# Expert selection: all queries first, the choices cut into pieces between the turned blocks, more low parts on GpSimd

## The chip, the cores and the metric

One Trainium2 chip, one of its cores, one launch. The time is the device time of one execution in microseconds (us). The engines have short names in the profile: PE is TensorE's matmul, PEld its weight load, DVE VectorE, ACT ScalarE, POOL GpSimd, SP SyncE, which issues most transfers.

## What is computed

A stack of blocks on one sequence of 256 tokens of width 1024: a gated delta rule, a gated MLP, a sliding-window attention, a second MLP, a block with a convolution and an attention, and at the end a layer of 16,384 experts. The change touches only that last layer:

```
q = (hc @ w_query).reshape(TOKEN_CHUNK, PEER_HEADS, 2, PEER_HALF)
sc = jnp.einsum('thpd,pnd->thpn', q, sub_keys)
vals, idx = lax.top_k(sc, PEER_TOPK)
cand = vals[:, :, 0, :, None] + vals[:, :, 1, None, :]
...
top_s, pos = lax.top_k(cand, PEER_TOPK)
gate = jax.nn.softmax(top_s, axis=-1)
u = expert_u[expert_idx]
act = jax.nn.gelu(jnp.einsum('thkd,td->thk', u, hc))
vv = expert_v[expert_idx]
return jnp.einsum('thk,thkd->td', gate * act, vv)
```

There are 8 heads, 128 keys in each half and 16 experts chosen for each head and token. The kernel gathers nothing: it computes the activation of all 16,384 experts for all tokens, as 128 blocks of 128 experts, and multiplies it with gates that are zero where an expert was not chosen.

## The kernel before

Every large product is made of three matmuls (`mm3`): each operand is split into a rounded high part and a low part, the rest. For weights ScalarE rounds the high part (`wh`) and VectorE or GpSimd subtracts to get the low part (`wl`). `low` deals the low parts out by a string for each stage, `LOW`: in the stage "top" it was "PPPD", three on GpSimd and one on VectorE, in turn.

The experts' layer, `peer`, has four stretches. In the first, "top", the queries are projected and scored (`peer_scores`, one call for each head), each head's best 16 of each half and of the pairs are found (`peer_topk`), the choices are turned into tables of keys and gates (`peer_tables`), and the first 64 blocks of `expert_u` are read, turned and multiplied (`u_pair`, two blocks at a time). In the second, "up", `u_pair` does the other 64 blocks while the gates of the first are made (`gates`, `gated`). The last two run over `expert_v`.

`u_pair` takes a pair of blocks. `u_turned` loads a block with four transfers into `raw` (three buffers), VectorE turns it with one stream transpose into `rt` (three buffers), and ScalarE casts the high part `wh` (three buffers). Then one of the two low parts goes to VectorE and one to GpSimd (`wl`, three buffers). A copy of one element for each partition ("the small copy" below) writes into GpSimd's `wl` first, so that GpSimd can't start ahead of that place in VectorE's order. 48 matmuls follow, and ScalarE takes the GELU of the pair.

The Tile framework orders each engine's instructions at build time by a planner with a timeline of its own, and prefers what stands earlier in the program. `InOrder` wraps an engine so that its instructions keep the program's order. Before, it was used from the stretch "up" on; in "top" the planner mixed VectorE's choices, tables, turns and low parts freely. The order in the program was `PEER`: the query and the choice of each head in turn, then the eight steps of the tables, then the 32 pairs of blocks.

Of the kernel before, what the change touches and what calls it, by code (L numbers as in the profile page):

```python
# [21 lines left out]
P = 128  # L22
T = 256
# [53 lines left out]
PEER = " ".join([f"q{i} k{i}" for i in range(8)] + [f"T{i}" for i in range(8)] + [f"u{i}" for i in range(32)])  # L77
# [7 lines left out]
LOW = dict(gdn="PPD", ffn="PD", swa="PPD", mix="P", tail="PPD", top="PPPD", up="PD", down="D", last="D")  # L85


class InOrder:

    def __init__(self, tc, eng):  # L90
        self.tc, self.eng = tc, eng

    def __getattr__(self, name):
        f = getattr(self.eng, name)
        return lambda *a, **kw: self.tc.keep_in_program_order(f(*a, **kw))


class Net:
# [746 lines left out]
    def peer_scores(self, us, kp, st, h):  # L845
# [22 lines left out]
        st[h] = sc = t(kp, [P, 2, 2, P], "sc", bufs=2)  # L868
# [4 lines left out]
    def peer_topk(self, kp, st, h):  # L873
        nc, t = self.nc, self.t

        def top16(v, i, src):
            nc.vector.max(v[:, 0:8], src)
            nc.vector.max_index(i[:, 0:8], v[:, 0:8], src)
            nc.vector.match_replace(src, v[:, 0:8], src, -3e38)
            nc.vector.max(v[:, 8:16], src)  # L880
            nc.vector.max_index(i[:, 8:16], v[:, 8:16], src)

        vals, idx, tops, pos = st["top"]
        sc = st.pop(h)
# [12 lines left out]

    def peer_tables(self, kp, st, i):

        nc, t = self.nc, self.t  # L900
        _, idx, tops, pos = st["top"]
        io = st["io"]
        b, step = i // 4, i % 4
        if step == 0:
            e = t(kp, [P, 8, 16], "e")
            tb = tops[:, b]
            nc.vector.tensor_tensor(e, tb, tb[:, :, 0:1].to_broadcast([P, 8, 16]), op=ALU.subtract)
            nc.scalar.activation(e, e, AF.Exp)
            z = t(kp, [P, 8], "z")
            nc.vector.tensor_reduce(z, e, axis=AX.X, op=ALU.add)  # L910
            nc.vector.reciprocal(z, z)
            nc.vector.tensor_tensor(e, e, z.unsqueeze(2).to_broadcast([P, 8, 16]), op=ALU.mult)
            st["sel"] = sel = t(kp, [P, 3, P], "sel")
            nc.vector.tensor_copy(sel[:, 2, :], e.rearrange("t h k -> t (h k)"))

            pb = pos[:, b].rearrange("t h k -> t (h k)")
            st["at"] = t(kp, [P, P], "row", BF16), t(kp, [P, P], "low", BF16)
            for o, arg, op in zip(st["at"], (3, 7), (ALU.logical_shift_right, ALU.bitwise_and)):
                ab = t(kp, [P, P], "ab", U32)
                nc.vector.tensor_scalar(ab, pb, arg, None, op0=op)  # L920
                nc.vector.tensor_copy(o, ab)
        elif step < 3:
            p, (row, low) = step - 1, st["at"]
            abf = t(kp, [P, P], "abf", BF16)
            if p == 0:
                nc.vector.tensor_scalar(abf, row, -1.0, 0.0, op0=ALU.add, op1=ALU.max)
            else:
                nc.vector.tensor_scalar(abf, row, 1.0, 8.0, op0=ALU.is_equal, op1=ALU.mult)
                nc.vector.tensor_add(abf, abf, low)
            ixf = t(kp, [P, 8, 16], "ixf", BF16)  # L930
            nc.vector.tensor_copy(ixf, idx[:, b, :, p, :])
            n = P // 4
            for i in range(4):
                c, h = slice(i * n, (i + 1) * n), slice(2 * i, 2 * i + 2)
                eq = t(kp, [P, n, 16], "eq16", BF16)
                nc.vector.tensor_tensor(eq, abf[:, c].unsqueeze(2).to_broadcast([P, n, 16]),
                                        io.unsqueeze(1).to_broadcast([P, n, 16]), op=ALU.is_equal)
                eh = eq.rearrange("t (h k) a -> t h k a", h=2)
                nc.vector.tensor_tensor(eh, eh, ixf[:, h].unsqueeze(2).to_broadcast([P, 2, 16, 16]), op=ALU.mult)
                nc.vector.tensor_reduce(st["sel"][:, p, c], eq, axis=AX.X, op=ALU.add)  # L940
        else:
            ps = self.ps()
            for p in range(3):
                nc.tensor.transpose(ps[:, p * P : (p + 1) * P], st["sel"][:, p, :], self.ident)
            tk = slice(b * P, (b + 1) * P)

            ku = t(kp, [P, 2, P], "ku", U32, bufs=1)
            nc.vector.tensor_copy(ku, ps[:, 0:256].rearrange("k (p t) -> k p t", p=2))
            for i, (arg, op) in enumerate(((4, ALU.logical_shift_right), (15, ALU.bitwise_and))):
                kk = t(kp, [P, 2, P], "kk", U32, bufs=1)  # L950
                nc.vector.tensor_scalar(kk, ku, arg, None, op0=op)
                nc.vector.tensor_copy(st["part"][:, i, :, tk], kk)
            gf = t(kp, [P, P], "gf")
            nc.vector.tensor_copy(gf, ps[:, 256:384])

            ex = t(kp, [P, P], "ex", U32)
            nc.vector.tensor_scalar(ex, gf.bitcast(U32), 0x7F800000, None, op0=ALU.bitwise_and)
            ef = ex.bitcast(F32)
            nc.vector.tensor_scalar(ef, ef, 2.0 ** -116, None, op0=ALU.max)
            nc.vector.tensor_scalar(st["two"][:, tk], ef, 2.0 ** -10, None, op0=ALU.mult)  # L960
            nc.vector.tensor_scalar(ex, ex, 0x7F800000, None, op0=ALU.bitwise_xor)
            nc.vector.scalar_tensor_tensor(gf, gf, 512.0, ef, op0=ALU.mult, op1=ALU.mult)
            nc.vector.tensor_copy(st["gate"][:, 0, tk], gf)
            nc.vector.tensor_sub(st["gate"][:, 1, tk], gf, st["gate"][:, 0, tk])

    def peer(self):
# [6 lines left out]
        with tc.tile_pool(name="ba", bufs=1, **tile_) as ba, tc.tile_pool(name="us", bufs=3, **tile_) as us, \  # L973
# [9 lines left out]
            ve = [nc.vector]  # L983

            def u_turned(j):
# [5 lines left out]
                ve[0].transpose(rt, raw)  # L991
# [5 lines left out]
            def u_pair(j, buf, between=None):  # L997
# [6 lines left out]
                if between:  # L1004
                    between()
# [526 lines left out]
```

## Time and profile before

| | |
|---|---|
| time, median of 3 runs | 1987.35 us (1985.11 to 1990.6) |
| the profiled execution: its time | 1986.34 us |
| its span | 1984.6 us |
| PE busy | 1848.3 us, 93% |
| DVE busy | 1438.0 us, 72% |
| ACT busy | 956.5 us, 48% |
| POOL busy | 671.8 us, 34% |
| mean granted TensorE clock | 0.973 |

The busy shares are means over the whole span. The stretch that the change touches lies between 1072 and 1376 us; what stands in its rows counts, not the mean.

### The profile page before, as it was taken

How to read it: one execution, taken by the hardware profiler on the slowest of the kernel's cores; microseconds unless marked ns; L12 is line 12 of the kernel's file. 1: busy time of each engine (PE TensorE's matmuls, PEld its weight loads, DVE VectorE, ACT ScalarE, POOL GpSimd, SP SyncE). 2: the span in 40 equal slices, each digit the busy share in tenths (PEclk: the TensorE clock that was granted, in tenths of full speed). 3: DMA queues.
4: the chain of work that ended last, by engine and by line, in shares of the span. 5: the costliest groups of instructions: out<-in, count | busy, mean ns of one | idle time of the engine just before them, and what ended most of it. 6: DMA issues, size and time to landing. Idle time of an engine off the chain costs nothing. (4 is left out here: it accounts for less than half of the span.)

```text
span 1984.6 us, 36930 instructions
## 1 busy us (share of the span) xinstructions
PE 1848.3 (93%) x14537; PEld 1747.2 (88%) x14537; DVE 1438.0 (72%) x2765; ACT 956.5 (48%) x1419; POOL 671.8 (34%) x309
## 2 busy tenths in 40 slices
PE   7979999999899999999968978889999999999998
PEld 7879999999889999989968968779999988887886
DVE  6786656666546666588864799999888878875555
ACT  5744435555656555456444533433333443444443
POOL 4444333444323444655634423334333300000000
PEclk9989999999899999999979999999999999999999
DMA  6454236666424666443524555555555555555665
GB/s 198 118 160 139 86 107 201 191 192 193 134 86 128 212 192 185 135 139 108 170 86 139 161 128 149 140 137 160 155 161 154 149 170 160 163 159 169 195 195 171
DMA packets 243435, 306.29 MB, mean 154 GB/s; under 512 B 26076, under 2 KB 213821, under 8 KB 243133
## 3 DMA queue, kind: packets, MB, share of 16 engines
q1 hardware_dynamic: 240864, 302.84, 50.6%
q8 instruction: 114, 1.87, 0.4%
q10 hardware_dynamic: 2237, 1.07, 0.2%
q14 instruction: 60, 0.49, 0.1%
q0 software_dynamic: 160, 0.02, 0.0%
HBM read 298.60 MB, written 4.74 MB: 153 GB/s over the span
## 5 line engine op out<-in xcount | busy, mean ns | idle before, releaser
L233 POOL TENSOR_TENSOR wl<-raw,wh 128x1024 fp32r<-128x1024 f32 (+1 forms) x196 | 470.5, 2404 | 558.5 <-ACT wh L242 499.8
L242 ACT CAST wh<-raw 128x1024 fp32r<-128x1024 f32 (+1 forms) x285 | 297.8, 1047 | 319.2 <-issue 111.9
L233 DVE TENSOR_TENSOR wl<-raw,wh 128x1024 fp32r<-128x1024 f32 x233 | 294.4, 1264 | 162.2 <-ACT wh L1103 103.4
L251 PE MATMUL pp<-xh,wl 128*128 128x256 f32 x1392 | 394.5, 284 | 16.4 <-DVE wl L1009 16.3
L249 PE MATMUL pp<-xh,wh 128*128 128x256 f32 x1392 | 394.9, 284 | 15.1 <-DVE kq L491 10.3
L251 PE MATMUL pa<-xh,wl 128*128 128x256 f32 (+1 forms) x1336 | 382.0, 286 | 19.7 <-DVE wl L1009 19.6
L249 PE MATMUL pa<-xh,wh 128*128 128x256 f32 (+1 forms) x1336 | 382.9, 287 | 14.4 <-ACT hT L304 6.2
L250 PE MATMUL pp<-xl,wh 128*128 128x256 f32 x1392 | 393.1, 282 | 2.1 <-DVE xl L374 2.1
L250 PE MATMUL pa<-xl,wh 128*128 128x256 f32 (+1 forms) x1336 | 381.1, 285 | 2.0 <-DVE xl L374 1.9
L251 PEld LDWEIGHTS pp<-xh,wl 128*128 128x128 f32 x1392 | 267.0, 192 | 18.8 <-DVE wl L1009 18.3
L249 PEld LDWEIGHTS pp<-xh,wh 128*128 128x128 f32 x1392 | 267.1, 192 | 16.9 <-issue 10.7
L251 PEld LDWEIGHTS pa<-xh,wl 128*128 128x128 f32 (+1 forms) x1336 | 257.3, 193 | 22.4 <-DVE wl L1009 22.4
L249 PEld LDWEIGHTS pa<-xh,wh 128*128 128x128 f32 (+1 forms) x1336 | 257.3, 193 | 16.5 <-ACT hT L304 6.6
L250 PEld LDWEIGHTS pp<-xl,wh 128*128 128x128 f32 x1392 | 266.8, 192 | 2.5 <-DVE xl L374 2.3
L1009 POOL TENSOR_TENSOR wl<-rt,wh 128x1024 fp32r<-128x1024 f32 x64 | 166.0, 2594 | 291.1 <-ACT wh L994 209.2
L250 PEld LDWEIGHTS pa<-xl,wh 128*128 128x128 f32 (+1 forms) x1336 | 257.3, 193 | 3.2 <-DVE xl L374 2.4
L994 ACT CAST wh<-rt 128x1024 fp32r<-128x1024 f32 x128 | 134.3, 1049 | 240.6 <-PE pa L250 104.2
L1103 ACT CAST wh<-raw 128x1024 fp32r<-128x1024 f32 x128 | 135.0, 1055 | 216.4 <-PE pa L1113 210.1
L1112 PE MATMUL pa<-wl,rt 128*128 128x512 f32 x512 | 201.7, 394 | 0.0
L1113 PE MATMUL pa<-wh,rt 128*128 128x512 f32 x512 | 199.5, 391 | 0.0
L1111 PE MATMUL pa<-wh,rt 128*128 128x512 f32 x512 | 164.6, 394 | 1.4 <-ACT rt L1097 1.4
L1154 POOL TENSOR_TENSOR fsb<-fsb,mhalf 128x1 f32<-128x1 f32 x2 | 1.1, 550 | 393.8 <-DVE fsb L1153 393.8
(433 smaller groups left out, 3575.4 us busy)
## 6 DMA issues: line engine op xcount, KB each, us to landing
raw<-in_peer_u_dram SPq DMA_DIRECT2D x512, 128.0 KB
raw<-in_peer_v_dram SPq DMA_DIRECT2D x128, 512.0 KB
raw<-in_ffn_w_up_dram SPq DMA_DIRECT2D x88, 512.0 KB
raw<-in_a_w_in_dram SPq DMA_DIRECT2D x48, 512.0 KB
raw<-in_ffn_w_down_dram SPq DMA_DIRECT2D x44, 512.0 KB
raw<-in_w_in_dram SPq DMA_DIRECT2D x44, 512.0 KB
raw<-in_a_w_out_dram SPq DMA_DIRECT2D x16, 512.0 KB
raw<-in_peer_w_query_dram SPq DMA_DIRECT2D x16, 512.0 KB
```

The source lines that it names most:

```text
L233: (self.nc.vector if order[self.turn % len(order)] == "D" else self.nc.gpsimd).tensor_tensor(out, raw, high, op=ALU.subtract)
L242: nc.scalar.copy(wh, raw)
L249: mm(out, wh, xh, start=start, stop=False, skip_group_check=skip)
L250: mm(out, wh, xl, start=False, stop=False, skip_group_check=skip)
L251: mm(out, wl, xh, start=False, stop=stop, skip_group_check=skip)
L994: nc.scalar.copy(uh.rearrange("p f (b e) -> p f b e", b=4), rv)
L1009: eng.tensor_tensor(lo.rearrange("p f (b e) -> p f b e", b=4), rv, high.bitcast(F32).rearrange("p f (b e) -> p f b e", b=4), op=ALU.subtract)
L1103: nc.scalar.copy(vh, raw)
L1111: nc.tensor.matmul(o, w2[:, 0, i, s], vh[:, c], start=first, stop=False)
L1112: nc.tensor.matmul(o, w2[:, 0, i, s], vl[:, c], start=False, stop=False)
L1113: nc.tensor.matmul(o, w2[:, 1, i, s], vh[:, c], start=False, stop=last)
L1154: nc.gpsimd.tensor_tensor(o, o, self.mhalf(), op=ALU.pow)
```

## The change

- All eight calls of `peer_scores` stand first; `sc` gets eight buffers instead of two, so that no score waits for a choice.
- `peer_topk` and `peer_tables` become generators. Each `yield` ends a piece and names its cost in us. `spend` takes pieces until their costs reach a sum: 14.0 us (`HEAD`) ahead of the first pair; in the first 16 pairs (`BOTH`) 1.0 us after each of the two turns; in the other 16 pairs 2.6 us once, after both turns. What is left is done at the end.
- In those first 16 pairs both low parts go to GpSimd, with a small copy for each. In the other 16, one is VectorE's and one GpSimd's, as before.
- VectorE keeps the program's order through the whole stretch "top", not only from "up" on.
- The low parts of the queries all go to GpSimd (`top="P"`).
- The two halves' searches in `peer_topk` alternate. In `peer_tables` the cast of the indices and a copy out of PSUM move from VectorE to ScalarE, the comparisons are done on 64 columns at a time instead of 32, and one copy falls away.

```diff
-LOW = dict(gdn="PPD", ffn="PD", swa="PPD", mix="P", tail="PPD", top="PPPD", up="PD", down="D", last="D")
+BOTH, HEAD, PIECE = 16, 14.0, (1.0, 2.6)
+LOW = dict(gdn="PPD", ffn="PD", swa="PPD", mix="P", tail="PPD", top="P", up="PD", down="D", last="D")
...
-        st[h] = sc = t(kp, [P, 2, 2, P], "sc", bufs=2)
+        st[h] = sc = t(kp, [P, 2, 2, P], "sc", bufs=8)
...
+        def top16(*of):
+            for s in (slice(0, 8), slice(8, 16)):
+                for v, _, src in of:
+                    ve.max(v[:, s], src)
+                for v, i, src in of:
+                    ve.max_index(i[:, s], v[:, s], src)
+                if s.start == 0:
+                    for v, _, src in of:
+                        ve.match_replace(src, v[:, s], src, -3e38)
...
+            top16(*[(vals[:, b, h, p], idx[:, b, h, p], sc[:, b, p, :]) for p in range(2)])
+            yield 2.5
...
+            ve.tensor_tensor(cand[:, 0:2, :], va[:, 0:1].unsqueeze(2).to_broadcast([P, 2, 8]),
+                             vb.rearrange("t (a b) -> t a b", a=2), op=ALU.add)
+            ve.tensor_tensor(cand[:, 2:17, :], va[:, 1:16].unsqueeze(2).to_broadcast([P, 15, 8]),
+                             vb[:, 0:8].unsqueeze(1).to_broadcast([P, 15, 8]), op=ALU.add)
+            top16((tops[:, b, h], pos[:, b, h], cand.rearrange("t a b -> t (a b)")))
+            yield 1.8
...
+        yield 1.2
...
+                ve.tensor_tensor(eq, abf[:, c].unsqueeze(2).to_broadcast([P, n, 16]),
+                                 io.unsqueeze(1).to_broadcast([P, n, 16]), op=ALU.is_equal)
+                yield 1.3
...
+                ve.tensor_tensor(eh, eh, ixs[p][:, h].unsqueeze(2).to_broadcast([P, 4, 16, 16]), op=ALU.mult)
+                ve.tensor_reduce(sel[:, p, c], eq, axis=AX.X, op=ALU.add)
+                yield 2.0
...
+        for p in range(3):
+            nc.tensor.transpose(ps[:, p * P : (p + 1) * P], sel[:, p, :], self.ident)
...
+        nc.scalar.copy(gf, ps[:, 256:384])
+        yield 0.7
+
+        ku = t(kp, [P, 2, P], "ku", U32, bufs=1)
+        ve.tensor_copy(ku, ps[:, 0:256].rearrange("k (p t) -> k p t", p=2))
...
+        yield 1.5
...
+        yield 1.6
...
-            ve = [nc.vector]
+            ve = InOrder(tc, nc.vector)
...
                 rb, bh = u_turned(j + 1)
+                if both:
+                    between()
                 ra, ah = u_turned(j)
                 al, bl = t(us, [P, DB, P], "wl", F32R), t(us, [P, DB, P], "wl", F32R)
-                if between:
-                    between()
-
-                ve[0].tensor_copy(al[:, 0, 0:1], bh[:, 0, 0:1])
-                for eng, lo, high, rv in ((ve[0], bl, bh, rb), (nc.gpsimd, al, ah, ra)):
+                between()
+
+                for lo in (al, bl) if both else (al,):
+                    ve.tensor_copy(lo[:, 0, 0:1], bh[:, 0, 0:1])
+                for eng, lo, high, rv in ((nc.gpsimd if both else ve, bl, bh, rb), (nc.gpsimd, al, ah, ra)):
...
-                self.play(PEER, q=lambda h: self.peer_scores(us, kp, st, h), k=lambda h: self.peer_topk(kp, st, h),
-                          T=lambda i: self.peer_tables(kp, st, i), u=lambda j: u_pair(2 * j, bufa))
+                for h in range(8):
+                    self.peer_scores(us, kp, st, h)
+
+                def pieces():
+                    for h in range(8):
+                        yield from self.peer_topk(ve, kp, st, h)
+                    for b in range(2):
+                        yield from self.peer_tables(ve, kp, st, b)
+
+                todo = pieces()
+
+                def spend(us_):
+
+                    while us_ > 0:
+                        us_ -= next(todo, 99)
+
+                spend(HEAD)
+                for i in range(J0 // 2):
+                    both = i < BOTH
+                    u_pair(2 * i, bufa, lambda: spend(PIECE[0] if both else PIECE[1]), both)
+                spend(99)
```

## Rows read from the trace of the kernel before

**Rows 1.** Stretch; busy us of PE, PEld, DVE, ACT, POOL; clock, DMA share, GB/s.

```profile
1144.00:1261.00 117.00, 91.75 (x717) 88.27 (x718) 115.98 (x334) 42.86 (x53) 34.81 (x16) 0.97 0.51 134
1261.00:1362.00 101.00, 84.75 (x664) 82.58 (x664) 99.79 (x130) 35.62 (x42) 36.31 (x14) 0.95 0.54 143
...
1382.00:1590.00 208.00, 208.00 (x1989) 206.57 (x1988) 182.92 (x305) 82.78 (x97) 79.17 (x31) 1.00 0.54 154
```

**Rows 2.** Waits between 1130 and 1362 us: us in total, times, longest.

```profile
PEld pa L251 <- DVE wl L1009: 22.4, 13, 2.7
```

**Rows 3.** ScalarE's timeline, the GELU of pairs 28, 29 and 31 of "top".

```profile
1359.19 0.59 ACT L1015 ACTIVATE bufa<-pa 128x512 f32<-128x512 f32 x1
1364.84 0.59 ACT L1015 ACTIVATE bufa<-pa 128x512 f32<-128x512 f32 x1
...
1375.47 0.60 ACT L1015 ACTIVATE bufa<-pa 128x512 f32<-128x512 f32 x1 [1.57 <-PE pa L251]
```

**Rows 4.** VectorE's timeline: start us, us, engine, line, operation, idle before.

```profile
1108.22 0.68 DVE L877 MAX8 vals<-sc 128x8 f32<-128x128 f32 x3 [4.01 <-ACT sc L870]
...
1124.30 0.86 DVE L877 MAX8 vals<-sc 128x8 f32<-128x128 f32 x4
...
1126.53 0.07 DVE L878 MATCH_VALUE_LOAD idx<-vals,sc 128x8 f32 x1
...
1139.37 2.35 DVE L991 STREAM_TRANSPOSE rt<-raw 128x1024 f32<-128x1024 f32 x2
...
1370.42 0.38 DVE L95 TENSOR_TENSOR a<-iot,part 128x512 bf16<-128x512 bf16 x1
1370.84 0.42 DVE L95 TENSOR_TENSOR a<-a,two 128x512 bf16<-128x512 bf16 x1
```

**Rows 5.** By source line: count, ns min/median/max, first and last start.

```profile
L1009 POOL TENSOR_TENSOR wl<-rt,wh x64: 2357/2407/3910, 1134.8 to 1581.2; 128x1024 fp32r<-128x1024 f32 x64
L1009 DVE TENSOR_TENSOR wl<-rt,wh x32: 1197/1226/3412, 1134.8 to 1367.0; 128x1024 fp32r<-128x1024 f32 x32
L892 DVE TENSOR_TENSOR cand<-vals x16: 125/156/2394, 1114.9 to 1235.9; 128x16 f32<-128x16 f32 x16
L894 DVE TENSOR_TENSOR cand<-vals x16: 267/271/1995, 1113.7 to 1235.9; 128x120 f32<-128x120 f32 x16
L936 DVE TENSOR_TENSOR eq<-abf,io x16: 644/678/2852, 1255.3 to 1334.2; 128x512 bf16<-128x512 bf16 x16
L939 DVE TENSOR_TENSOR eq<-eq,ixf x16: 377/412/2634, 1258.3 to 1338.4; 128x512 bf16<-128x512 bf16 x16
```

**Rows 6.** Timelines of GpSimd and VectorE: a low part on each at once, twice.

```profile
1236.50 2.40 POOL L1009 TENSOR_TENSOR wl<-rt,wh 128x1024 fp32r<-128x1024 f32 x1 [5.14 <-DVE tops L877]
...
1236.60 3.38 DVE L1009 TENSOR_TENSOR wl<-rt,wh 128x1024 fp32r<-128x1024 f32 x1
...
1313.54 1.21 DVE L1009 TENSOR_TENSOR wl<-rt,wh 128x1024 fp32r<-128x1024 f32 x1
1314.68 2.93 DVE L939 TENSOR_TENSOR eq<-eq,ixf 128x512 bf16<-128x512 bf16 x2
...
1313.82 3.16 POOL L1009 TENSOR_TENSOR wl<-rt,wh 128x1024 fp32r<-128x1024 f32 x1 [7.34 <-ACT wh L994]
```

**Rows 7.** Timelines of GpSimd and VectorE: two low parts of GpSimd in a row.

```profile
15.14 4.75 POOL L233 TENSOR_TENSOR wl<-raw,wh 128x1024 fp32r<-128x1024 f32 x2 [4.95 <-DMA rows<-in_ffn_conv_w_dram]
...
15.20 2.39 DVE L211 TENSOR_TENSOR wfg<-colsv 128x8 f32<-128x8 f32 x1
17.51 0.15 DVE L215 TENSOR_TENSOR wf<-colsv 128x8 f32<-128x8 f32 x1
17.59 2.98 DVE L374 SCALAR_TENSOR_TENSOR xl<-hT,colsn,xh 128x256 fp32r<-128x256 f32 x2
```

**Rows 8.** Timelines of VectorE and GpSimd: a small copy and the low part it releases.

```profile
1134.55 0.14 DVE L1007 CAST wl<-wh 128x1 fp32r<-128x1 f32 x1
...
1134.83 3.45 POOL L1009 TENSOR_TENSOR wl<-rt,wh 128x1024 fp32r<-128x1024 f32 x1 [6.76 <-DVE wl L1007]
```

More of the change, by code (lines that the diff above doesn't have):

```diff
@@ L902, in peer_tables @@
         io = st["io"]
[L903 to L923, printed above, removed]
+        sel = t(kp, [P, 3, P], "sel")
@@ new lines, in peer_tables @@
+        pb = pos[:, b].rearrange("t h k -> t (h k)")
+        at = t(kp, [P, P], "row", BF16), t(kp, [P, P], "low", BF16)
+        ixs = [t(kp, [P, 8, 16], f"ixf{p}", BF16) for p in range(2)]
+        for p in range(2):
+            nc.scalar.copy(ixs[p], idx[:, b, :, p, :])
+        e = t(kp, [P, 8, 16], "e")
+        tb = tops[:, b]
+        ve.tensor_tensor(e, tb, tb[:, :, 0:1].to_broadcast([P, 8, 16]), op=ALU.subtract)
+        nc.scalar.activation(e, e, AF.Exp)
+        for o, arg, op in zip(at, (3, 7), (ALU.logical_shift_right, ALU.bitwise_and)):
+            ab = t(kp, [P, P], "ab", U32)
+            ve.tensor_scalar(ab, pb, arg, None, op0=op)
+            ve.tensor_copy(o, ab)
@@ L924, in peer_tables @@
+        yield 1.2
+        row, low = at
+        for p in range(2):
             abf = t(kp, [P, P], "abf", BF16)
             if p == 0:
-                nc.vector.tensor_scalar(abf, row, -1.0, 0.0, op0=ALU.add, op1=ALU.max)
+                ve.tensor_scalar(abf, row, -1.0, 0.0, op0=ALU.add, op1=ALU.max)
             else:
-                nc.vector.tensor_scalar(abf, row, 1.0, 8.0, op0=ALU.is_equal, op1=ALU.mult)
-                nc.vector.tensor_add(abf, abf, low)
-            ixf = t(kp, [P, 8, 16], "ixf", BF16)
@@ L931, in peer_tables @@
[L931 to L934, printed above, removed]
-                eq = t(kp, [P, n, 16], "eq16", BF16)
[L936 to L964, printed above, removed]
@@ new lines, in peer_tables @@
+                ve.tensor_scalar(abf, row, 1.0, 8.0, op0=ALU.is_equal, op1=ALU.mult)
+                ve.tensor_add(abf, abf, low)
+            n = P // 2
+            for i in range(2):
+                c, h = slice(i * n, (i + 1) * n), slice(4 * i, 4 * i + 4)
+                eq = t(kp, [P, n, 16], "eq16", BF16)
+                ve.tensor_tensor(eq, abf[:, c].unsqueeze(2).to_broadcast([P, n, 16]),
+                                 io.unsqueeze(1).to_broadcast([P, n, 16]), op=ALU.is_equal)
+                yield 1.3
+                eh = eq.rearrange("t (h k) a -> t h k a", h=4)
+                ve.tensor_tensor(eh, eh, ixs[p][:, h].unsqueeze(2).to_broadcast([P, 4, 16, 16]), op=ALU.mult)
+                ve.tensor_reduce(sel[:, p, c], eq, axis=AX.X, op=ALU.add)
+                yield 2.0
@@ new lines, in peer_tables @@
+        z = t(kp, [P, 8], "z")
+        ve.tensor_reduce(z, e, axis=AX.X, op=ALU.add)
+        ve.reciprocal(z, z)
+        ve.tensor_tensor(sel[:, 2, :].rearrange("t (h k) -> t h k", h=8), e, z.unsqueeze(2).to_broadcast([P, 8, 16]),
+                         op=ALU.mult)
+        ps = self.ps()
+        for p in range(3):
+            nc.tensor.transpose(ps[:, p * P : (p + 1) * P], sel[:, p, :], self.ident)
+        tk = slice(b * P, (b + 1) * P)
+        gf = t(kp, [P, P], "gf")
+        nc.scalar.copy(gf, ps[:, 256:384])
@@ new lines, in peer_tables @@
+        yield 0.7
+        ku = t(kp, [P, 2, P], "ku", U32, bufs=1)
+        ve.tensor_copy(ku, ps[:, 0:256].rearrange("k (p t) -> k p t", p=2))
+        for i, (arg, op) in enumerate(((4, ALU.logical_shift_right), (15, ALU.bitwise_and))):
+            kk = t(kp, [P, 2, P], "kk", U32, bufs=1)
+            ve.tensor_scalar(kk, ku, arg, None, op0=op)
+            ve.tensor_copy(st["part"][:, i, :, tk], kk)
+        yield 1.5
+        ex = t(kp, [P, P], "ex", U32)
+        ve.tensor_scalar(ex, gf.bitcast(U32), 0x7F800000, None, op0=ALU.bitwise_and)
@@ L966, in peer @@
+        ef = ex.bitcast(F32)
+        ve.tensor_scalar(ef, ef, 2.0 ** -116, None, op0=ALU.max)
+        ve.tensor_scalar(st["two"][:, tk], ef, 2.0 ** -10, None, op0=ALU.mult)
+        ve.tensor_scalar(ex, ex, 0x7F800000, None, op0=ALU.bitwise_xor)
+        ve.scalar_tensor_tensor(gf, gf, 512.0, ef, op0=ALU.mult, op1=ALU.mult)
+        ve.tensor_copy(st["gate"][:, 0, tk], gf)
+        ve.tensor_sub(st["gate"][:, 1, tk], gf, st["gate"][:, 0, tk])
+        yield 1.6
     def peer(self):
@@ L990, in u_turned @@
                 rt = t(us, [P, D], "rt", bufs=3)
-                ve[0].transpose(rt, raw)
+                ve.transpose(rt, raw)
                 rv = rt.rearrange("p (b f e) -> p f b e", b=4, f=DB)
@@ L1053, in one_hot @@
                 eq(a8, 0, 8, part[:, 0, 1])
[L1054 removed]
+                ve.tensor_tensor(a8, a8, two[:, tk].unsqueeze(1).to_broadcast([P, 8, N]), op=ALU.mult)
                 eq(a16, 0, 16, part[:, 1, 1])
```

40 lines of the change are left out of this document (13 added, 27 removed).

## The prediction

> **What bounds the kernel now.** I read the stretches first. After 1382 us PE is busy without a gap, 208 of 208 us [rows 1]: there nothing that VectorE saves is worth anything, and the change leaves that part as it is. Between 1144 and 1362 us it is the other way round: VectorE is busy 215.8 of 218 us and PE 176.5 [rows 1]. The waits say on what PE waits there: on the low parts that VectorE makes, up to 2.7 us at a time [rows 2]. So the stretch is worth what VectorE's chain is worth, until that chain gets shorter than PE's. PE's own pace shows at the end of "top", where the choices are done: a pair each 5.65 us [rows 3].
>
> Then I read how busy VectorE really is. A low part takes 1.2 us there and up to 3.41; the short add of 16 columns takes 0.16 us and up to 2.39; the comparisons and products of the tables show the same [rows 5]. The long ones stand beside a low part of GpSimd: that runs from 1236.50 to 1238.90, and VectorE's, begun at 1236.60, takes 3.38, which is the rest of GpSimd's and its own 1.2 [rows 6]. The reverse is there as well: GpSimd's takes 3.16 instead of 2.4 where VectorE's began 0.28 ahead, and VectorE's next product then waits in its turn [rows 6]. Such operations exclude each other; turns and searches never lengthen (two turns take 2.35 [rows 4]). So GpSimd's work has a price for VectorE, and the change doubles it in 16 pairs.
>
> **The change, part by part.** The sum is made against the profiled execution: 1986.34 us, a span of 1984.6 and 1.7 around it; the median of the runs is 1.0 above it. Positions are those of its span. A pair is counted from its last small copy.
>
> *Prices.* A turn is 1.15 (two take 2.35 and overlap the next by 0.08). A search for the best 8 is 0.2 (four take 0.86); a find or a replace has a load of 0.07 ahead of it and is 0.27 [rows 4]. An operation that needs the one ahead of it starts 0.04 after its end instead of 0.08 before: 0.12 lost for each link (the last two of [rows 4]). The piece called 2.5 has 4 searches, 4 finds and 2 replaces, alternating between two halves, so no link shows: 2.4. The piece called 1.8 has two adds (0.35 [rows 5]), 2 searches, 2 finds, a replace and 4 links: 2.0. A quarter of a table is twice the 512 columns of [rows 5]: comparison 1.14, product 0.6, sum 1.14 (estimated like the comparison), links 0.2, together 3.1.
>
> *Queries first, sixteen low parts on GpSimd.* Before, the first choice begins at 1108.2 after 4.0 us without work, on the first score [rows 4]. Nothing that makes that score gets earlier, so I keep 1108.2; a score held up by the missing buffers only concerned later heads. GpSimd makes the queries' low parts in 2.4 each, PE uses one half-head in 5.65/2 = 2.8: hidden under PE, and if that cover failed, 0.4 at most for each of four more, 1.6 us. `HEAD` takes seven pieces until the sum passes 14.0: 4 × 2.4 + 3 × 2.0 = 15.6. Their adds meet GpSimd's low parts: between 0 and 2 × 2.4 for each of four pieces with adds (pair 0's included); GpSimd being busy most of the time then, I take 1.0 each, 4.0.
>
> *A pair with both low parts on GpSimd.* VectorE's order is turn, piece, turn, piece, two small copies: 2.3 + 2.4 + 2.0 + 0.15 = 6.85. Before, it had a low part in place of half of the choices. As the head took seven pieces, the piece behind the first turn is always the one with the adds. It comes 1.22 us after the small copy; GpSimd starts 0.28 after it [rows 8] and holds until 2.7. So the adds wait 1.45, and all behind them: second turn, second piece, the copies, and with these the next pair's low parts. Whether the second add waits again, for GpSimd's second low part, is the open price: 0 or 2.4. The one place with two short VectorE operations behind two low parts of GpSimd in a row has the first waiting 2.39, the second through in 0.15 and the third held [rows 7]; the product of [rows 6] behind a long operation was held at once. The adds are like the former, so I take 0: 8.3 a pair. The Trainium skill ("SBUF — State Buffer", "Who interferes with whom") says that of a VectorE operation with two SBUF inputs and a GpSimd one that reads SBUF, the first to issue has the shared ports for its whole length. Its first wait agrees with [rows 6]; by it the second add would be held too, a rival below.
>
> PE needs 5.65 and GpSimd 4.8 of the 8.3, so neither sets the pace. VectorE ends the first piece's pair at 1108.2 + 15.6 + 4.0 + 6.85 = 1134.7; twelve more pairs, 99.6, lead to 1234.3, with all choices done.
>
> *Pairs 13 to 15* have the tables' comparison behind the first turn and the product behind the second. In 13 the short step ahead of the comparison waits to 2.7, GpSimd gets in between (a link, as in [rows 6]), the comparison starts at 5.15, and the pair takes 9.4; 14 has the comparison at 2.7 and the product held to 6.25, 8.2; 15 is like 13 with one more step, 9.7. To 1261.6.
>
> *Pairs 16 to 22*: low part 1.14, turns 2.3, small copy, pieces. VectorE's low part follows the small copy at once and wins; GpSimd's ends 3.6 after it, when the turns are just over: 0.15 of waiting. A pair with one quarter is 6.75; pair 16 still meets the two low parts of 15, 8.1; pair 18 has the second table's start, 7.9. In 17 and 22 VectorE needs the transposed choices, and PE, whose order puts them behind the pair it is in, is up to 3.2 us away: between 0 and 3.2, I take the middle: 9.2 each. 8.1 + 9.2 + 7.9 + 3 × 6.75 + 9.2 = 54.7, to 1316.3.
>
> *The last nine* have no pieces: 3.7 us of VectorE a pair against PE's 5.65, so PE sets them. 1316.3 + 1.2 + 10 × 5.65 = 1374.0, against 1375.5 before [rows 3]. The casts moved to ScalarE lie beside its 40 % of work [rows 1]; without them VectorE would have 0.2 for each of six.
>
> The sum is −1.5 us: 1985. VectorE gives up twenty low parts, but pays about as much for waits, links and nine pairs in which it is idle.
>
> **The rivals.** *Held twice.* The second add waits for GpSimd's second low part in each of twelve pairs: 12 × 2.4 = 28.8, a pair of 10.7, 2014. For it: the product of [rows 6], held at once; against it: [rows 7]. The Trainium skill's rule above is on its side. It decides as soon as GpSimd's second low part has begun when the first add ends.
>
> *Not held.* The adds run ahead of GpSimd: it needs only start 1.2 us after the small copies instead of 0.28. For it: GpSimd's waits end on ScalarE's cast or on VectorE's search as often as on the small copy [rows 6, 8]; against it: with a pair of 8.3 us the casts are long done. Then 12 × 1.45, some 10 in pairs 13 to 15, 2.7 in pair 16 and the 4.0 of the head fall away, 34 us: 1951. An order of PE that takes the transposes early, or a first score before 1108, would give parts of it.
>
> *The order doesn't hold as written*, or VectorE waits for a transfer ahead of a turn. In the trace its turns don't wait, and between two uses of a `raw` buffer lie three turns; I give it no chance of its own.
>
> **How the numbers follow.** No change that a measurement could tell (0.3 %, 6 us) is what the sum says; held once is likeliest, 0.45, with a range of its own from 1970 to 1998, since the pair's 8.3 stands twelve times and 0.8 us of error in it is 10. Of that 0.18 is faster, 0.16 the same, 0.11 slower. Not held, whole or in part, has 0.30, held twice 0.25. Faster 0.48, same 0.16, slower 0.36. The range from 1955 to 2012 leaves out a third of each of the two outer cases.
>
> **What would show it.** In the changed kernel's trace: VectorE's first search near 1108; GpSimd with two low parts in a row from 0.3 us behind the small copies; the first add of nearly every pair taking about 1.6 us, the second 0.3 (2.7 if held twice, both short if not held); the GELUs of pairs 1 to 12 some 8.3 us apart, the last nine 5.65; the stretch after 1382 as long as before. It would be wrong by other means if PE's clock fell for whole pairs: with 2.65 us idle in each 8.3, against 41 in 218 before, a granted clock far below the 0.95 to 0.97 of [rows 1] would make a pair of up to 11.3.

## The result, and the profile after

The changed kernel takes 1999.11 us (median of 6, 1995.82 to 2001.21) against 1988.97 for the kernel before (1985.11 to 1992.13): a ratio of 1.0057, interval 1.0043 to 1.0071. It is slower by 0.6 %, where no change or a small gain was forecast; the time is inside the range. Its profiled execution, the fastest of the six, took 1995.82 us, a span of 1994.0.

The stretches of the changed kernel (columns as in [rows 1]): the first twelve pairs, and the part after "top".

```profile
1134.70:1242.50 107.80, 82.95 (x583) 79.31 (x582) 97.08 (x350) 35.98 (x47) 57.92 (x24) 0.87 0.38 117
...
1394.00:1600.00 206.00, 206.00 (x1970) 204.67 (x1967) 181.00 (x302) 81.49 (x95) 78.41 (x31) 1.00 0.55 154
```

Against [rows 1]: behind "top" PE is busy without a gap as before. In the pairs the granted clock is 0.87, not 0.97, and VectorE, which was hardly ever idle there, now is for a tenth of the time.

Next VectorE's timeline: the small copies that open pairs 0, 1, 2, 3 (two at once where a row says x2), 12, 15 and 22, with the two adds of the pair that follows the copies of 1150.96.

```profile
1134.59 0.19 DVE L99 CAST wl<-wh 128x1 fp32r<-128x1 f32 x2
1142.73 0.19 DVE L99 CAST wl<-wh 128x1 fp32r<-128x1 f32 x2
1150.96 0.19 DVE L99 CAST wl<-wh 128x1 fp32r<-128x1 f32 x2
1152.23 1.58 DVE L99 TENSOR_TENSOR cand<-vals 128x16 f32<-128x16 f32 x2
...
1159.07 0.14 DVE L99 CAST wl<-wh 128x1 fp32r<-128x1 f32 x1
1161.24 0.15 DVE L99 CAST wl<-wh 128x1 fp32r<-128x1 f32 x1 [2.03 <-PE pa L255]
...
1242.44 0.21 DVE L99 CAST wl<-wh 128x1 fp32r<-128x1 f32 x2
...
1268.74 0.20 DVE L99 CAST wl<-wh 128x1 fp32r<-128x1 f32 x2
...
1327.01 0.15 DVE L99 CAST wl<-wh 128x1 fp32r<-128x1 f32 x1
```

The first copy stands at 1134.59, forecast for 1134.7. The pairs behind it take 8.14 and 8.23 us, forecast 8.3, and the adds are held for 1.58 together: this far the sum holds. Then a pair takes 10.2, because its second copy waits 2.03 us for PE. The sum by stretches, measured and forecast: pairs 1 to 12 107.9 and 99.6; 13 to 15 26.3 and 27.3; 16 to 22 58.3 and 54.7; from there to the last GELU, below, 59.6 and 57.7. That is the whole difference of 12.6 us at the end of "top"; behind it this execution took 1.7 us less than the profiled one of the kernel before. ScalarE's timeline, where [rows 3] had 1375.47:

```profile
1386.56 0.60 ACT L1032 ACTIVATE bufa<-pa 128x512 f32<-128x512 f32 x1 [1.85 <-PE pa L255]
```

VectorE's waits between 1105 and 1395 us (in total, times, longest), and in a second view the copies' idle time between 1144 and 1254:

```profile
DVE wl L99 <- PE pa L255: 17.3, 10, 2.1
DVE wl L99 <- PE pp L255: 6.8, 4, 1.7
DVE ku L99 <- ACT gf L959: 6.7, 2, 3.4
```

```profile
L99 DVE CAST wl<-wh 128x1 fp32r<-128x1 f32 x24 | 2.8, 141 | 8.3 <-PE pa L255 6.6 <-PE pp L255 1.7
```

Nothing waited like this in the forecast: 8.3 us at copies in the twelve pairs and 6.7 us at the transposed choices of pairs 17 and 22. That the twelve pairs lost just these 8.3 us against the forecast is partly chance: one pair was 2.2 us longer, since its second add was held as well, and the other eleven, without their waits, were 0.2 us shorter each than the 8.3 forecast.

### The profile page after: what moved, and what is told of

The parts are those of the page before. It is cut to its first block, busy times and chain, and to the rows that moved or that the text cites. A ratio compares the mean times of both kernels' runs of the same rounds, so it can differ in the third digit from the quotient of the medians.

```text
span 1994.0 us, 36940 instructions
## 1 busy us (share of the span) xinstructions
PE 1859.3 (93%) x14537; PEld 1758.9 (88%) x14537; DVE 1408.2 (71%) x2729; ACT 961.7 (48%) x1427; POOL 721.3 (36%) x329
## 5 line engine op out<-in xcount | busy, mean ns | idle before, releaser
L237 POOL TENSOR_TENSOR wl<-raw,wh 128x1024 fp32r<-128x1024 f32 (+1 forms) x200 | 479.9, 2403 | 547.9 <-ACT wh L246 504.1
L255 PE MATMUL pa<-xh,wl 128*128 128x256 f32 (+1 forms) x1336 | 388.0, 291 | 24.3 <-DVE wl L99 12.7
L253 PE MATMUL pp<-xh,wh 128*128 128x256 f32 x1392 | 394.1, 283 | 16.3 <-DVE kq L495 10.2
L253 PE MATMUL pa<-xh,wh 128*128 128x256 f32 (+1 forms) x1336 | 388.9, 291 | 20.7 <-ACT wh L1009 9.5
L237 DVE TENSOR_TENSOR wl<-raw,wh 128x1024 fp32r<-128x1024 f32 x229 | 289.5, 1264 | 155.7 <-ACT wh L1139 101.8
L254 PE MATMUL pa<-xl,wh 128*128 128x256 f32 (+1 forms) x1336 | 386.6, 290 | 0.0
L1026 POOL TENSOR_TENSOR wl<-rt,wh 128x1024 fp32r<-128x1024 f32 x80 | 206.2, 2586 | 260.9 <-ACT wh L1009 135.8
L255 PEld LDWEIGHTS pa<-xh,wl 128*128 128x128 f32 (+1 forms) x1336 | 263.0, 197 | 27.1 <-DVE wl L99 13.7
L253 PEld LDWEIGHTS pa<-xh,wh 128*128 128x128 f32 (+1 forms) x1336 | 263.5, 197 | 23.0 <-ACT wh L1009 10.3
L254 PEld LDWEIGHTS pa<-xl,wh 128*128 128x128 f32 (+1 forms) x1336 | 263.2, 197 | 1.2 <-issue 0.6
L99 DVE STREAM_TRANSPOSE rt<-raw 128x1024 f32<-128x1024 f32 x128 | 153.1, 1224 | 2.0 <-POOL wl L1026 1.4
```

Source lines behind the costliest of these rows:

```text
L237: (self.nc.vector if order[self.turn % len(order)] == "D" else self.nc.gpsimd).tensor_tensor(out, raw, high, op=ALU.subtract)
L253: mm(out, wh, xh, start=start, stop=False, skip_group_check=skip)
L254: mm(out, wh, xl, start=False, stop=False, skip_group_check=skip)
L255: mm(out, wl, xh, start=False, stop=stop, skip_group_check=skip)
L1026: eng.tensor_tensor(lo.rearrange("p f (b e) -> p f b e", b=4), rv, high.bitcast(F32).rearrange("p f (b e) -> p f b e", b=4), op=ALU.subtract)
```

## The experiments

Ratios are to the kernel before on the same chip; the changed kernel's is 1.0057.

**The parts of the change.** With `BOTH, HEAD, PIECE = 0, 14.0, (1.0, 2.6)`, all but the moved low parts:

> BOTH is 0: each pair has one low part on VectorE and one on GpSimd, all else as in the changed kernel (order as written, pieces behind the second turn). VectorE's pair is a low part of 1.15, two turns, a piece of each kind and a small copy, 8.1 us, and GpSimd's single low part is through when the adds come. Theory B (the adds' wait behind two low parts is what the change lost): 12 x (8.85 - 8.1) = 9 us less, near 1990, and the adds 0.3 us. Theory A (PE idle some 2.5 us at a time in each pair, and its clock falls): the pair stays near 8.8 and the granted clock near 0.87, 1999 within 4 us, though the adds wait no longer.

0.9950 (0.9934 to 0.9965), 21 us less than the changed kernel; granted clock 0.93 in the first twelve pairs, the pairs 7.9 us. More than theory B gave, and theory A is wrong on it. The reverse, the moved low parts alone in the kernel before:

```diff
-ve[0].tensor_copy(al[:, 0, 0:1], bh[:, 0, 0:1])
-for eng, lo, high, rv in ((ve[0], bl, bh, rb), (nc.gpsimd, al, ah, ra)):
+both = buf is bufa and j < 32
+for lo in (al, bl) if both else (al,):
+    ve[0].tensor_copy(lo[:, 0, 0:1], bh[:, 0, 0:1])
+for eng, lo, high, rv in ((nc.gpsimd if both else ve[0], bl, bh, rb), (nc.gpsimd, al, ah, ra)):
```

> The kernel before, with its own order, where the first sixteen pairs have both low parts on GpSimd; nothing else of the change. If the moved low parts are what the change loses by (their holds on VectorE's adds and products, PE left waiting 2.4 us per low part, its lower clock): slower than before by 5 to 20 us, 1995 to 2010. Rival (they are worth VectorE's 16 x 1.15 us, and the loss comes from the order as written): 10 to 18 us faster, 1971 to 1979.

1.0071 (1.0048 to 1.0093), slower by 14 us as expected. So all the rest of the change (the order as written, the pieces, the queries first) gains 0.5 %; the low parts on GpSimd lose it and more.

**The adds' place.** `HEAD` 12.0 in place of 14.0:

> HEAD is 12.0 in place of 14.0: the head takes six pieces, so the piece with the two adds stands behind the second turn of each pair, not behind the first. It then begins some 4.9 us after the small copies, when GpSimd's two low parts (0.3 to 5.1 us) are nearly through. Theory A (the adds' wait lengthens the pair, and PE, left idle for longer at a time, falls to its lower clock and lengthens it again): the first add takes 0.3 to 0.5 in place of 1.4 us, a pair of VectorE's 7.1, the granted clock in the first twelve pairs back above 0.94 from 0.87; 12 x (8.85 - 7.1) = 21 us less, near 1978. Theory B (only the adds' wait counts, the clock is a bystander): 12 x 1.2 = 14 less, near 1985, the granted clock still near 0.87. Rival (the second low part now holds the second add, or GpSimd gets later): within 4 us of 1999.

0.9952 (0.9935 to 0.9970): theory A's time, but not its way. The first add takes 0.27 us, yet the pairs' GELUs go 5.9 and 10.7 us by turns and the clock is 0.93.

**The transposes.** `yield 2.7` in place of `yield 0.7` behind `gf`:

> The step that copies the transposed choices is placed a pair later (2.7 in place of 0.7 behind the transposes), so that VectorE does not reach it while PE still has the pair ahead of the transposes. Theory C (the two pairs of 13.6 and 13.8 us come from this wait and the stall and lower clock that it leaves on PE): each becomes about 8, in all 9 to 11 us less, near 1989, and PE's two idle stretches of 5.3 us are gone. Rival (VectorE then waits for the same transposes one pair later, or the lower clock comes in the tables' pairs anyway): less than 4 us.

0.9986 (0.9970 to 1.0002), 14 us less than the changed kernel, somewhat more than expected. What went, in the changed kernel, PE's and VectorE's timelines:

```profile
1283.45 0.27 PE L956 MATMUL pm<-c_head,sel 128*128 128x128 f32 x1
...
1289.26 0.58 PE L255 MATMUL pa<-xh,wl 128*128 128x256 f32 x1 [5.30 <-DVE wl L99]
...
1284.44 0.42 DVE L99 CAST ku<-pm 128x256 uint32<-128x256 f32 x1 [3.35 <-ACT gf L959]
```

PE takes the transpose behind the pair it is in, VectorE stands 3.35 us for it, and then PE 5.30 for VectorE. With both edits together:

> HEAD 12.0 and the later copies of the transposed choices together, all else as in the changed kernel. If the two losses are separate (theories A and C): 21 us from the first and some 8 from the second, whose one long stall is left there, near 1971. Rival (the second falls to the first, as the pair with the transposes is only stalled once there): near 1979.

0.9925 (0.9900 to 0.9951): some 5 us on top of the first edit's gain, between the two forecasts.

**The clock.** Sixteen matmuls behind each of the first sixteen pairs:

```diff
+if both:
+    fill = self.ps()
+    for k in range(16):
+        nc.tensor.matmul(fill[:, 0:T], xh[:, k % DB, 0:P], xh[:, k % DB, :], start=True, stop=True)
```

> Behind each of the first sixteen pairs PE does 16 more matmuls of 256 columns, 1.9 us at full clock, into a bank that nobody reads: 5.65 + 1.9 = 7.6 us of the pair's 8.3. VectorE and GpSimd do what they do in the changed kernel. Theory A (the pairs' excess over 8.3 us comes from PE's lower clock, which follows its long idle stretches): the granted clock between the first and the thirteenth pair rises from 0.87 to 0.97 or more, the pairs are 8.3 us apart each, not 7 and 11 by turns, 7 us less there and some 3 in the next four: near 1990. Theory B (the clock is a bystander): the same time, 1999 within 3 us, at whatever clock; if PE's lower clock stays, 7.6 becomes 15 and it is slower by up to 50 us.

1.0003 (0.9986 to 1.0019). Copies and the stretch of twelve pairs:

```profile
1165.03 0.20 DVE L99 CAST wl<-wh 128x1 fp32r<-128x1 f32 x2
1173.29 0.20 DVE L99 CAST wl<-wh 128x1 fp32r<-128x1 f32 x2
```

```profile
1139.90:1238.10 98.20, 95.96 (x800) 94.14 (x799) 95.58 (x351) 35.80 (x47) 58.68 (x24) 1.00 0.45 129
```

From the third on every pair takes 8.27 us, at full clock. All that theory A said came; it is still not shown by this, as will be seen. A fourth buffer for the low parts instead (`more` holds the pool `kp` during "top"; `eq16` has one buffer to pay for it):

```diff
-al, bl = t(us, [P, DB, P], "wl", F32R), t(us, [P, DB, P], "wl", F32R)
+al = t(us, [P, DB, P], "wl", F32R)
+bl = t(more[0], [P, DB, P], "wl4", F32R, bufs=1) if more and j % 4 else t(us, [P, DB, P], "wl", F32R)
```

> The changed kernel with a fourth buffer for the low parts in the turned blocks' pairs (paid for with one buffer fewer for the tables' comparison), so that a small copy no longer needs the buffer that PE still reads. Theory A in its later form (PE at its lower clock frees the buffers late, VectorE's small copies wait 8.3 us for it in the first twelve pairs, and the rest of the order with them): the copies 8.3 us apart throughout, 8 to 11 us less over the first sixteen pairs, near 1990, even at a granted clock of 0.87. Rival (PE's own matmuls at the lower clock and its two stops set the slow pairs): the pairs stay at 7 and 11 by turns, 1999 within 4 us.

0.9997 (0.9983 to 1.0011):

```profile
1154.00 0.19 DVE L99 CAST wl<-wh 128x1 fp32r<-128x1 f32 x2
1162.21 0.20 DVE L99 CAST wl<-wh 128x1 fp32r<-128x1 f32 x2
1170.36 0.20 DVE L99 CAST wl<-wh 128x1 fp32r<-128x1 f32 x2
```

```profile
1137.70:1236.80 99.10, 78.89 (x575) 75.87 (x574) 96.97 (x351) 35.58 (x46) 57.83 (x24) 0.90 0.42 127
```

8.2 us a pair although the clock is 0.90: in these pairs the clock costs only through the buffer that a copy waits for.

**Spread evenly.** Three kernels with a head of ten pieces, all pieces behind the second turn, what is spent over 2.8 us a pair carried on, and the late copy:

```diff
-    while us_ > 0:
-        us_ -= next(todo, 99)
+    left[0] += us_
+    while left[0] > 0:
+        left[0] -= next(todo, 99)
```

`BOTH` is 32, 17 and 0:

> All 32 pairs have both low parts on GpSimd; the head takes ten pieces, so that VectorE is done with them about when PE is done with the queries (1137 us); in a pair all pieces stand behind the second turn, and what a pair spends over 2.8 us is kept for the next, so most pairs have one piece; the copies of the transposed choices come a pair later. Theory A (long waits of PE and its lower clock are what the change lost; where VectorE's pair is below PE's 5.65, PE is not left idle and keeps its clock): a pair of choices takes VectorE 2.3 + 2.4 + 0.15 + 0.3 = 5.2, below PE's 5.65; from 1141 some 20 pairs at 5.65 and, in the tables, some eight at 8 since the product waits there for GpSimd's second low part: last GELU near 1341 in place of 1386.6, 45 us less than the changed kernel, near 1955; granted clock above 0.96. Rival (GpSimd's 4.8 us, lengthened by VectorE's adds and products, or the waits of the adds make the pair 8 as before): 1985 to 1999.

> As the kernel with all low parts on GpSimd, but only the first 17 pairs have both there, the others one on VectorE: the tables' comparisons and products then do not meet two low parts. First 17 pairs 5.65 (PE's), the other 15 VectorE's 1.15 + 2.3 + 0.1 + 2.75 = 6.3: last GELU near 1141 + 96 + 15 x 6.3 = 1332, 54 us less than the changed kernel, near 1945 (theory A). Rival as there: 1985 to 1999.

> As the kernel with all low parts on GpSimd, but each pair has one low part on VectorE. VectorE's pair is 1.15 + 2.3 + 0.1 + 2.75 = 6.3 throughout, and PE has about 0.65 us idle in each. Theory A (only long waits close together bring the lower clock): last GELU near 1141 + 31 x 6.3 = 1337, 50 us less than the changed kernel, near 1950, granted clock above 0.97. Rival (any idle time of PE lowers its clock in these pairs): the clock near 0.9, pairs of 7, near 1970.

1.0157 (1.0138 to 1.0177), 0.9988 (0.9978 to 0.9999) and 0.9812 (0.9793 to 0.9831). The last came as expected; the first, 2021.4 us, missed by 66 us and lies beyond its rival's range too; the second missed by 43 and fell into the rival's. VectorE's timeline of the first:

```profile
1195.29 1.25 DVE L99 STREAM_TRANSPOSE rt<-raw 128x1024 f32<-128x1024 f32 x1 [1.30 <-POOL wl L1024]
...
1199.59 0.13 DVE L99 CAST wl<-wh 128x1 fp32r<-128x1 f32 x1
1202.79 0.15 DVE L99 CAST wl<-wh 128x1 fp32r<-128x1 f32 x1 [3.07 <-PE pp L255]
```

The second turn waits for the buffer that GpSimd's first low part still reads, and in one pair of three the second copy again waits for PE. Which pairs these are, the list of the program's instructions tells. GpSimd's of the changed kernel, pairs 1 and 2:

```
L1026 TENSOR_TENSOR wl_1746_13128<-rt_1739_13106,wh_1740_13108 128x1024
L1026 TENSOR_TENSOR wl_1745_13127<-rt_1743_13123,wh_1744_13125 128x1024
L1026 TENSOR_TENSOR wl_1755_13219<-rt_1753_13215,wh_1754_13217 128x1024
L1026 TENSOR_TENSOR wl_1756_13220<-rt_1749_13198,wh_1750_13200 128x1024
```

PE uses 1746 before 1745 and 1756 before 1755 (`bl` first). In pair 2, and in every even one from 0 to 10, GpSimd makes `al` first ("reversed" from here on): only VectorE is kept in the program's order. In its first twelve pairs every copy that waits opens the pair behind a reversed one. The filled kernel has but one reversed pair, the first, so the fill had changed two things. The kernel with a fourth buffer has one in four, that of 1162.21 among them, and the next copies stand 8.15 us on all the same; its 12 us can't be put down to the buffer alone.

**GpSimd's order.** Kept as written, with no other edit (in PE's list two matmuls of every second pair move by half a pair with it, VectorE's stays the same):

```diff
+po = InOrder(tc, nc.gpsimd)
-for eng, lo, high, rv in ((nc.gpsimd if both else ve, bl, bh, rb), (nc.gpsimd, al, ah, ra)):
+for eng, lo, high, rv in ((po if both else ve, bl, bh, rb), (po if both else nc.gpsimd, al, ah, ra)):
```

> The changed kernel with GpSimd's low parts kept in the order as written, so that the block that PE multiplies first is always split first (in the changed kernel every second pair has them the other way round). Theory G (the reversed order makes PE stand some 5 us at a time in every second pair; its lower clock and the late buffers follow from that): PE stops once in each pair, some 2.6 us, the granted clock in the first twelve pairs is 0.95 or more, the pairs are 8.3 us each, 8 to 12 us less than the changed kernel, near 1989. Rival (VectorE's long pair alone leaves PE idle enough to lose its clock, whatever the order): clock near 0.87, 1999 within 4 us.

1.0006 (0.9992 to 1.0020), 10 us less than the changed kernel:

```profile
1156.46 0.20 DVE L99 CAST wl<-wh 128x1 fp32r<-128x1 f32 x2
...
1164.67 0.20 DVE L99 CAST wl<-wh 128x1 fp32r<-128x1 f32 x2
```

```profile
1140.20:1237.40 97.20, 78.13 (x586) 75.68 (x585) 95.07 (x350) 35.84 (x47) 58.07 (x24) 0.93 0.44 130
```

Pairs of 8.2, no copy waits. The clock is 0.93, not the 0.95 expected, and costs nothing. Now `reversed(lows)` in each of the first sixteen pairs, so that `al` is always made first:

> The changed kernel with GpSimd's low parts kept reversed in all of its first sixteen pairs, so that the block that PE multiplies first is always split second. Theory G in its last form (a reversed pair is a loop of its own: small copies, 0.3, two low parts 4.8, then both of PE's halves before the buffer that the next pair's copy needs is free, some 10.4 us at full clock, more at the lower): every pair 10.4 us or more, 12 x 2.1 = 25 us more than with the order as written (1990), near 2016 or above. Rival (a reversed pair is only late because its neighbour is not, or only through the lower clock): 1999 within 6 us.

1.0140 (1.0118 to 1.0161), 2018.9 us. Pair 3, on VectorE, GpSimd and PE:

```profile
1165.94 0.15 DVE L99 CAST wl<-wh 128x1 fp32r<-128x1 f32 x1 [1.37 <-PE pa L255]
...
1166.92 4.82 POOL L99 TENSOR_TENSOR wl<-rt,wh 128x1024 fp32r<-128x1024 f32 x2 [5.54 <-ACT wh L1010]
...
1171.79 0.58 PE L255 MATMUL pp<-xh,wl 128*128 128x256 f32 x1 [1.57 <-POOL wl L99]
...
1176.25 0.15 DVE L99 CAST wl<-wh 128x1 fp32r<-128x1 f32 x1 [1.32 <-PE pp L255]
```

10.3 us from copy to copy, from the third pair on, as forecast; but the loop was not the one I had written. PE starts as GpSimd ends, and the copy follows 4.5 us later: one half at a clock lower for most of it, not both halves at full clock. In pairs 2 to 10 PE's and VectorE's lists are the same here and in the kernel with the order as written, and only GpSimd's order differs: 10.3 us a pair against 8.2.

The first two pairs, reversed as well, take 8.1 and 8.8 us, and no copy waits behind them. Pair 1, on PE and VectorE:

```profile
1150.52 0.39 PE L253 MATMUL pa<-xh,wh 128*128 128x256 f32 x1 [1.06 <-ACT wh L1010]
...
1152.60 0.39 PE L255 MATMUL pa<-xh,wl 128*128 128x256 f32 x1 [1.58 <-POOL wl L99]
...
1155.60 0.20 DVE L99 CAST wl<-wh 128x1 fp32r<-128x1 f32 x2
```

The order and PE's stops are those of pair 3, which has 1.06 and 1.57 us. But the granted clock is 1.00 in pair 1 and 0.84 in pair 3, and both copies go 3.0 us after PE's start without a wait. So the reversed order alone does not make the copy wait; it takes the lower clock too. Why PE keeps its clock in pair 1 and not in the later ones, behind the same stops, stays open.

The last kernel of this kind, reversed in every second pair and filled:

> The 16 filling matmuls behind each of the first sixteen pairs, with GpSimd's low parts kept reversed in every second pair, as the changed kernel has them. If the lower clock is a link that the loss needs: PE, filled, stands 1.5 us at most in two pairs, its clock stays near 1.00, VectorE's small copies stay 8.3 us apart, and the time is that of the other filled kernel, near 1990. If the reversed order costs by itself, without the clock (buffers freed late by PE's later start): copies 8.3 and 9.5 or more by turns, 1997 or slower.

1.0044 (1.0027 to 1.0060). It reads as if the order cost by itself at full clock, but it doesn't tell that. VectorE, GpSimd and PE in one reversed pair:

```profile
1173.73 0.20 DVE L99 CAST wl<-wh 128x1 fp32r<-128x1 f32 x2
1184.09 0.15 DVE L99 CAST wl<-wh 128x1 fp32r<-128x1 f32 x1 [1.97 <-PE pa L255]
...
1174.08 4.91 POOL L99 TENSOR_TENSOR wl<-rt,wh 128x1024 fp32r<-128x1024 f32 x2 [3.35 <-ACT wh L1010]
...
1179.28 2.20 PE L1038 MATMUL pm<-xh 128*128 128x256 f32 x17
1181.32 0.28 PE L255 MATMUL pa<-xh,wl 128*128 128x256 f32 x1
```

The filling matmuls lie ahead of the pair's and hold it from 1179.0, when GpSimd is done, to 1181.3; the copy goes 2.8 us later, when PE's first half is done. The fill made this wait. It does show the loop: the copy follows the first half, whatever made that late.

**With the order kept, elsewhere.** In the kernel with all low parts on GpSimd, and in the one with the adds second and the late copy:

> The kernel with all 32 pairs' low parts on GpSimd, those kept in the order as written. Theory G: its pairs of 13 to 15 us, one in three, are gone; VectorE's second turn still waits for GpSimd's first low part (it needs that one's buffer) and its adds for the second: 6.3 and 7.1 us by turns, 8 in the tables, last GELU near 1362 in place of 1411, near 1972. Rival (the buffers, with two low parts on GpSimd, are what makes it slow): within 10 us of 2021.

> The kernel with the adds behind the second turn and the later copies of the transposed choices, with GpSimd's low parts kept in the order as written, PE not filled. Theory G: its pairs are 7.1 to 7.3 us each, not 5.9 and 10.7 by turns, 10 to 13 us less than 1973.4, near 1962, granted clock 0.97 or more. Rival: 1973 within 4 us.

1.0018 (1.0005 to 1.0031), 28 us better than without the order and 21 us short of what was expected: what holds that one further, beside the wait of the second turn, stays open. The second, 0.9840 (0.9819 to 0.9861), came as expected: it is the changed kernel repaired at its three places. Its copies, the adds of a pair, and the stretch of its first twelve:

```profile
1152.13 0.20 DVE L99 CAST wl<-wh 128x1 fp32r<-128x1 f32 x2
...
1156.87 0.60 DVE L99 TENSOR_TENSOR cand<-vals 128x16 f32<-128x16 f32 x2
...
1159.27 0.20 DVE L99 CAST wl<-wh 128x1 fp32r<-128x1 f32 x2
```

```profile
1137.90:1223.50 85.60, 72.76 (x596) 70.32 (x595) 83.31 (x363) 35.28 (x45) 56.83 (x24) 1.00 0.53 153
```

7.13 us a pair at full clock. The same kernel without the kept order, with half the fill:

> The adds behind the second turn and the later copies of the transposed choices (HEAD 12.0, 2.7), with 8 more matmuls of 256 columns behind each of the first sixteen pairs, 0.95 us at full clock, into a bank that nobody reads. PE then has 6.6 of VectorE's 7.1 us. Theory A (that kernel's pairs are 5.9 and 10.7 by turns, not 7.1, only because of PE's lower clock): granted clock near 1.00, the first twelve pairs 7.1 each in place of 8.2, 10 to 13 us less than 1973.4, near 1961. Rival (VectorE's chain or the buffers make the 8.2): the same or slower, 1973 or more.

0.9896 (0.9874 to 0.9918), about half of the gain expected: GELUs 6.6 to 7.4 us apart at first, then two of 11.9 and 13.0, at the only two pairs behind the first in which GpSimd's order was reversed.

**The fastest.** Two more of the kernel with one low part on VectorE:

> The evenly spread kernel with one low part on VectorE in each pair, but a head of 14.0 in place of 20.0: seven pieces ahead of the first turn, not ten. The first pair is then turned and split by 1138 us, when PE is done with the queries, so PE does not stand some 4 us there; three more pieces lie beside the pairs. Expected 3 to 5 us less than 1952.9, near 1949. Rival (VectorE sets the pairs, and what the head does not do they do): the same within 2 us.

> One low part on VectorE in each pair, a head of 14.0, pieces spread with 3.1 us for each pair, so that they end within the 32 pairs (with 2.8 the last 5 us stood behind the last pair, and PE then stood 3.6 us and fell to its lower clock for 10 us). Against the kernel with a head of 20.0 (1952.9): the first pair 5 us earlier, no wait behind the last: 1946 to 1950. Rival (VectorE sets the pairs all through): 1953 within 3 us.

0.9852 (0.9834 to 0.9870) and 0.9812 (0.9793 to 0.9831). Both forecasts missed; neither kernel beats the 0.9812 of the one with the head of 20.0. The first pair does come earlier. In the former the last GELU comes 7 us earlier too, and as much is lost behind it, where PE stands and falls in clock; in the latter the pairs take back what the start saved, as its rival had it. The two kernels at 0.9812 are the fastest, 1.9 % faster than the kernel before.

## Why the prediction was wrong

*Right*: the start (1134.59 for 1134.7), though by luck in part, since the first search came 1.3 us late and the head's adds waited 2.5 us in place of 4.0; the first add held once, the second let through; 8.3 us for a pair (8.1 to 8.3 wherever nothing else waits); pairs 13 to 15 and the last nine's pace; behind "top" nothing. "Held twice" happened in one pair of twelve; "not held", in a pair, only where the adds were placed elsewhere. With GpSimd's order kept, the time is what the sum said, within the noise (1.0006).

*The step that failed* is "PE needs 5.65 and GpSimd 4.8 of the 8.3, so neither sets the pace". It sets shares side by side that stand in one loop: a copy, GpSimd's low parts up to the one that PE needs first, PE's first half (the block `j + 1` of the pair), the buffer that this half frees, the next pair's copy into it. At full clock the half takes some 2.8 us, and the loop is 0.3 + 2.4 + 2.8 = 5.5 in the order as written and 0.3 + 4.8 + 2.8 = 7.9 reversed, both under 8.2. At the lower clock the half takes 5.1, and the reversed loop is 0.3 + 4.8 + 5.1 = 10.2. In the changed kernel, pairs 0 and 2, both reversed, on GpSimd and then on PE:

```profile
1134.86 4.81 POOL L1026 TENSOR_TENSOR wl<-rt,wh 128x1024 fp32r<-128x1024 f32 x2 [5.76 <-DVE wl L99]
1151.23 4.78 POOL L1026 TENSOR_TENSOR wl<-rt,wh 128x1024 fp32r<-128x1024 f32 x2 [3.28 <-DVE wl L99]
```

```profile
1139.73 0.39 PE L255 MATMUL pp<-xh,wl 128*128 128x256 f32 x1 [0.94 <-POOL wl L1026]
...
1142.31 0.28 PE L255 MATMUL pp<-xh,wl 128*128 128x256 f32 x1
1142.43 0.28 PE L253 MATMUL pp<-xh,wh 128*128 128x256 f32 x1
...
1153.49 0.39 PE L253 MATMUL pp<-xh,wh 128*128 128x256 f32 x1 [2.05 <-ACT wh L1009]
1153.71 0.28 PE L254 MATMUL pp<-xl,wh 128*128 128x256 f32 x1
1156.07 0.58 PE L255 MATMUL pa<-xh,wl 128*128 128x256 f32 x1 [2.08 <-POOL wl L1026]
1156.45 0.42 PE L253 MATMUL pa<-xh,wh 128*128 128x256 f32 x1
1156.66 0.42 PE L254 MATMUL pa<-xl,wh 128*128 128x256 f32 x1
...
1160.72 0.41 PE L255 MATMUL pa<-xh,wl 128*128 128x256 f32 x1
```

In pair 0 PE goes on at a matmul per 0.12 us (2.4 GHz): its first half runs from 1139.73 to 1142.6, and the copies of 1142.73 do not wait. In pair 2 it has stood 2.05 and 2.08 us with two matmuls between (the next pair's first two, which stand ahead in PE's list), comes back at one per 0.21 (1.2 GHz), and its first half runs from 1156.07 to 1161.1; then the copy of 1161.24 goes. So the slow pairs need three things: the reversed order (kept as written: 10 us back), the lower clock in the first half (without it no wait, in pair 0 here and in pair 1 of the kernel reversed in all pairs), and no buffer to spare (with a fourth no wait even behind a reversed pair at the lower clock). In the order as written a first half of 5.1 us ends 7.8 after the copies, so the clock of 0.93 cost nothing there. I had named the clock as what could make the forecast wrong, without a chance; I had taken GpSimd's order for that of the source, and had given the rival "the order doesn't hold as written" no chance either.

The filled kernel alone would have made the clock the cause; the run that only kept the order shows that without the reversed pairs the loss is gone. That the clock is needed rests on the pairs reversed at full clock and on the arithmetic of the loop; the run meant to test it does not tell, since its fill made PE late by itself.

*Mis-sized*: the transposes. "Between 0 and 3.2, I take the middle: 9.2 each" measured 11.1 each, a little beyond the far end (10.8): VectorE waited 3.4 each time. PE's stop of 5.3 us behind it came on top; the late copy gives back 14 us.

The Trainium skill ("SBUF — State Buffer", "Who interferes with whom") has the operation that issues first keep the shared ports for its length. The first add agrees: 1.35 to 1.43 us in the twelve pairs, where an add that met no low part took 0.16. By that rule I had let the second add be held too, as a rival; it took 0.27 us in eleven of the twelve pairs, just as GpSimd's second low part began, and 2.54 in one.

## What to carry to other kernels

Where engines pass few buffers round, add up the loop, from one release of a buffer to the next, with each engine's order as it is issued and at the lower clock too; busy shares that all fit say nothing of it. If one engine is kept in the program's order, look at the order of the engines that feed on it. An experiment that changes the program may change a queue's order elsewhere: compare the lists of instructions before reading the time.

## What the hardware showed that I had not expected

Of two short VectorE operations behind two GpSimd low parts in a row the first waits to the end of the first one (the row of 1152.23, 1.58 us for both adds), and in eleven pairs of twelve the second passes. In the kernel reversed in all pairs PE fell to 1.2 GHz behind stops of 1.06 and some 1.6 us with two matmuls between, in every pair from the third to the twelfth (granted clock 0.84 in pair 3), but not behind the same stops in the second; in the one with the adds second, the late copy and the order kept it stayed at 1.00 over twelve pairs with one stop of 1.0 to 1.5 us in each from the third on.
